# Denominators of latent attention from a column of ones in a third value product, rope tables in three transfers, a later load of x

## The chip, the cores and the metric

One Trainium2 chip, of which the kernel uses one core. The metric is the device time of one execution in microseconds, and a kernel is compared by its median over several executions.

## What is computed

The reference runs two transformer blocks over one sequence of 1024 tokens of width 1024, all in float32. The first mixes a pooling path and a sliding-window attention and adds the result to x; the second is a hybrid of latent attention (MLA, 8 heads, keys and queries of 96, values of 64) and three groups of dilated attention, with gates, an output product and a final norm. Cut to the part at issue:

```python
def mla_attention(c_q, c_kv, k_rope, positions, q_norm_g, kv_norm_g, w_uq, w_ukv):
    q = (rmsnorm_2(c_q, q_norm_g) @ w_uq).reshape(B, S, MLA_HEADS, MLA_QK_DIM)
    q = jnp.concatenate([q[..., :64], rope(q[..., 64:], positions)], axis=-1) * 96 ** -0.5
    kv = (rmsnorm_2(c_kv, kv_norm_g) @ w_ukv).reshape(B, S, MLA_HEADS, 64 + 64)
    k_nope, v = kv[..., :64], kv[..., 64:]
    k_pe = rope(k_rope[:, :, None, :], positions)          # shared by the heads
    s = jnp.einsum('bqhd,bkhd->bhqk', q, k)                # no mask
    return jnp.einsum('bhqk,bkhd->bqhd', jax.nn.softmax(s, axis=-1), v)

def first_block(x, ...):
    ...
    y = jnp.concatenate([pool_out, attn_out], axis=-1) @ w_out
    return x + rmsnorm(y, norm_post)

def rope(t, positions):      # cos and sin of position x frequency, 32 frequencies for 64, 16 for 32
    ...
```

## The kernel before

Every float32 product is made of three fast ones. A tensor is split into a high part, rounded to the matmul's type (an ACT copy), and a low part, the rest (a DVE subtraction, `sub_lo`, L119); then high x high, high x low and low x high are summed in one PSUM bank. Such a group of three is called a triple below (`mm3_lane`, lines L360 to L362). Projections go by tiles of 128 outputs by 512 tokens, 8 triples each.

The program has stages in this order: the first block (its output product with `y_lane`, which also loads x as `xt` and adds it, and which calls `rope_tables` at the second token tile); projections and dilated attention of the second block; the latent projections (`c_lane`: eight token tiles of c_q, c_kv and k_rope, then `ct_lane`, which transposes each normalized tile `cn` on PE); `uq_lane` and `ukv_lane`, which make queries, keys and values; the latent attention; the two output products into a merge, and the last product. The order on PE is written by a planner while the program is built: each lane is a generator that yields the events it needs, `Flow.run` always steps the lane of highest priority whose events are due by its own clock (0.23 us a product of 512 columns), and `Ring` objects stand for buffers. A lane can be put off with `at(us)` or with a later event; both put the numbers 20.0 and 2.5 into the latent projections. `stream_lane`, of the lowest priority, fills the rest with projections of the gates (`gate_item`, triples on `pp`); in the latent attention a meter, `pace`, lets through so many of its triples per key block. The order on ACT, DVE, POOL and SP comes from the scheduler of the tile framework, which also holds an instruction back until its buffer is free.

In the latent attention four lanes run over heads, halves of 512 queries and 8 blocks of 128 keys. `max_lane` multiplies keys and queries once to find each query's maximum, transposes it and sends it as `mt` by DMA into a row of the queries. `exp_lane` makes the scores in three products (L1646 to L1648) and, on ACT, the exponential (L1653) and its high part `E` (L1654); DVE makes the low part `pl` (L119). `hi_lane` multiplies `E` by the 128 columns of `vm` that hold the low and the high part of the values (L1683), and `lo_lane` multiplies `pl` by the high part and a column of ones beside it (L1696), into a second bank. So per key block there are two value products. The sum over keys of `E` and `pl` together is what divides the output. The share of `pl` is row 64 of `lo_lane`'s bank. The share of `E` is summed apart: POOL adds the eight `E` of a half head (L1664, L1666) into `acc`, and `key_sums` splits `acc` into a high and a low part `ehl` (ACT L1588, DVE L119), multiplies both with `ones` on PE (L1593, L1594, bank `psd`), copies the row (L1598) and stores it in `den_d`.

At the end of a half head the banks are copied and added: ACT copies `ot` (L1703), DVE adds (L1704), ACT copies `ou` (L1705), DVE adds again (L1706), and SP stores `ot` in `a_d` and ACT the row of `ou` in `den_d`. `ot`, `ou`, `den` and `mt` all come from one pool of two buffers:

```python
                nc.scalar.copy(t[0:64], o[64:128])
                nc.vector.tensor_tensor(out=t[0:64], in0=o[0:64], in1=t[0:64], op=ALU.add)
                nc.scalar.copy(u[0:65], o2[0:65])
                nc.vector.tensor_tensor(out=t[0:64], in0=t[0:64], in1=u[0:64], op=ALU.add)
```

`finish`, once per two heads, loads both rows of denominators, adds them, takes the reciprocal, spreads it by DMA, and multiplies the output on POOL. The merge then loads that as `raw`, splits it into `at`, and multiplies it by w_o (the first product on `at` ends the latent part).

`rope_tables` makes one cosine and two sine tables of 32 frequencies by 1024 positions, as tiles of 128 rows (4 quarters of the positions by 32 frequencies) by 256, and stores each to `cs_d` in four transfers (L579). `tables` reads 32-row slices for the dilated attention, and the lines behind L1368 16-row slices for the latent attention.

Of the kernel before, what the change touches and what calls it, by code (L numbers as in the profile page):

```python
# [14 lines left out]
S = 1024  # L15
# [52 lines left out]
def hybrid_kernel(  # L68
# [467 lines left out]
    cs_d = tc.dram_tile([3, 32, S], F32, name="cs_d")  # L536

    def rope_tables():
# [434 lines left out]
    def y_lane(t):  # L973
# [7 lines left out]
        xt = C("xt")  # L981
        nc.sync.dma_start(xt, x[128 * t:128 * t + 128, :])
# [32 lines left out]
    a_d = tc.dram_tile([512, S], F32, name="a_d")  # L1015
    ag_d = tc.dram_tile([512, S], F32, name="ag_d")
    den_d = tc.dram_tile([2, 8, S], F32, name="den_d")
# [43 lines left out]

    def z_item(o, dst, j, evs):
# [307 lines left out]
    for r in range(2):  # L1370
        nc.sync.dma_start(qtab[64 + 16 * r:80 + 16 * r], cs_d[0, 0:32:2])
        nc.sync.dma_start(qtab[96 + 16 * r:112 + 16 * r], cs_d[2 - r, 0:32:2])
        nc.sync.dma_start(ktab[16 * r:16 * r + 16], cs_d[0, 0:32:2])
        nc.sync.dma_start(ktab[32 + 16 * r:48 + 16 * r], cs_d[2 - r, 0:32:2])
# [26 lines left out]
    def c_lane():  # L1401
        yield (at(20.0),)
        for t in range(8):
# [17 lines left out]
            F.add(ct_lane(t, cn, Ev(slot.t + 2.5)), 4)  # L1421
# [104 lines left out]
    ones = cst.tile([128, 1], F32R, name="ones")  # L1526
    nc.vector.tensor_scalar(out=ones, in0=ident[:, 0:1], scalar1=0.0, scalar2=1.0, op0=ALU.mult, op1=ALU.add)
# [3 lines left out]
    den_ev = [[Ev(), Ev()] for _ in range(8)]  # L1531
# [51 lines left out]
    def key_sums(e, h, half, ready):  # L1583
        yield (ready, R.P)
        Pslot = R.P.take()
        ehl = P_p.tile([128, 2, 512], F32R, tag="P", name="ehl")
        eh, el = ehl[:, 0], ehl[:, 1]
        nc.scalar.copy(eh, e)  # L1588
        sub_lo(nc.vector, el, e, eh)
        yield (R.S, Ev(F.chain(("a", 0.6), ("v", 1.3)) + 3.0))  # L1590
        slot = R.S.take()
# [296 lines left out]
```

## Time and profile before

| | us |
|---|---|
| runs | 1740.76, 1731.06, 1731.16 |
| median | 1731.16 |
| the profiled execution | 1742.75 |
| its span, first to last instruction | 1740.7 |
| its mean granted clock of TensorE | 0.977 of full speed |

A row of groups names the line, the engine, the operation, what it writes and reads, the shapes and the count; then busy time, the mean duration, and the idle time of the engine just before with what ended it. In a timeline row the first number is the start, the second the duration, and what stands in brackets is how long the engine was idle before it and what released it. Line numbers are those of the kernel before.

### The profile page before, as it was taken

The numbers are of one execution on the slowest core, as the hardware profiler recorded it, in microseconds if no ns is written. First come the engines' busy times: TensorE is split into PE (matmuls) and PEld (weight loads), VectorE is DVE, ScalarE is ACT, GpSimd is POOL, SyncE is SP. The second block draws the span as 40 slices with busy tenths as digits, with TensorE's granted clock in tenths as the row PEclk, the third lists the DMA queues.
The fourth block names the chain that finished last, engine by engine and source line by source line (L and its number), as shares of the span: only waits on it lengthen the run. The fifth ranks groups of instructions, "written<-read, shape, count | busy, mean of one in ns | idle before, by whom it ended". The sixth has DMA issues, their size and how long they took to land.

```text
span 1740.7 us, 22397 instructions
## 1 busy us (share of the span) xinstructions
PE 1647.7 (95%) x7892; PEld 1355.4 (78%) x7892; DVE 1016.3 (58%) x1912; ACT 798.0 (46%) x1659; POOL 394.2 (23%) x336
## 2 busy tenths in 40 slices
PE   6999997999999999999999988899998989999998
PEld 6888876788788788888888777887766767777786
DVE  6587693453566646665555663365676767545432
ACT  5465533332455545655444442315665656742121
POOL 2000020000000000000000444452566566622200
PEclk9999998999999999999999999999999999999999
DMA  6111224534443443334345668354223231378542
GB/s 193 49 49 39 69 91 141 157 116 121 98 96 80 100 118 87 80 88 116 94 101 115 156 168 215 89 173 150 57 76 103 58 104 48 103 243 289 160 139 80
DMA packets 214092, 200.59 MB, mean 115 GB/s; under 512 B 50451, under 2 KB 177299, under 8 KB 212444
## 3 DMA queue, kind: packets, MB, share of 16 engines
q1 hardware_dynamic: 210780, 188.55, 39.4%
q10 hardware_dynamic: 3200, 10.62, 1.7%
q8 instruction: 62, 1.02, 0.2%
q14 instruction: 50, 0.41, 0.1%
HBM read 124.73 MB, written 48.11 MB: 99 GB/s over the span
## 4 chain that ended last, share of the span: by engine, by line
PE 46%; DMA 8%; DVE 7%; ACT 5%; SPq 4%; issue 3%; POOL 2%; DVEq 0%; POOLq 0%; ACTq 0%
PE pp L360 8%; PE pp L362 8%; PE pp L361 8%; DMA rsw<-rt 3%; SPq L1185 2%; PE pso L493 2%; PE y L361 2%; PE y L362 2%; PE y L360 2%; PE pss L1646 1%; PE pso L1696 1%; PE pst L463 1%; PE pss L1648 1%; PE pss L1647 1%; PE pso L1683 1%
## 5 line engine op out<-in xcount | busy, mean ns | idle before, releaser
L360 PE MATMUL pp<-Hh,whi 128*128 128x512 f32 x1248 | 504.7, 404 | 11.8 <-DVE pg L588 5.9
L362 PE MATMUL pp<-Hh,wlo 128*128 128x512 f32 x1248 | 492.8, 395 | 0.0
L361 PE MATMUL pp<-Hl,whi 128*128 128x512 f32 x1248 | 492.0, 394 | 0.0
L360 PEld LDWEIGHTS pp<-Hh,whi 128*128 128x128 f32 x1248 | 238.6, 191 | 57.7 <-DVE pg L588 6.8
L362 PEld LDWEIGHTS pp<-Hh,wlo 128*128 128x128 f32 x1248 | 237.0, 190 | 52.5
L361 PEld LDWEIGHTS pp<-Hl,whi 128*128 128x128 f32 x1248 | 238.2, 191 | 42.4
L127 ACT CAST whi<-wraw 128x1024 fp32r<-128x1024 f32 (+1 forms) x108 | 109.2, 1011 | 198.7 <-PE pp L361 95.6
L119 DVE TENSOR_TENSOR wlo<-wraw,whi 128x1024 fp32r<-128x1024 f32 (+1 forms) x108 | 135.2, 1252 | 100.4 <-ACT whi L127 91.0
L1666 POOL TENSOR_TENSOR acc<-acc,E 128x512 f32<-128x512 f32 x96 | 132.0, 1375 | 84.3 <-ACT E L1654 81.5
L443 ACT ACTIVATE P<-P,nm 128x256 f32<-128x256 f32 (+2 forms) x256 | 118.8, 468 | 59.4 <-DVE nm L438 59.2
L119 DVE TENSOR_TENSOR pl<-pss,E 128x512 fp32r<-128x512 f32 x128 | 86.9, 686 | 67.4 <-ACT E L1654 66.4
L1653 ACT ACTIVATE pss<-pss 128x512 f32<-128x512 f32 x128 | 74.9, 588 | 70.7 <-PE pss L1648 62.3
L1567 DVE TENSOR_REDUCE mx<-pst 128x1 f32<-128x512 f32 x128 | 83.6, 682 | 19.1 <-PE pst L1565 18.6
L119 DVE TENSOR_TENSOR pl<-pst,ph 128x512 fp32r<-128x512 f32 (+2 forms) x120 | 75.3, 639 | 32.0 <-ACT ph L469 31.4
L432 DVE CUSTOM_DVE_ANT_0 P<-pss,cc 128x256 f32<-128x256 f32 (+2 forms) x192 | 62.9, 369 | 45.8 <-PE pss L1145 45.7
L167 POOL TENSOR_TENSOR rs<-ms,mhalf 128x1 f32<-128x1 f32 (+1 forms) x40 | 25.0, 626 | 273.0 <-DVE ms L165 272.9
L469 ACT CAST ph<-pst 128x512 fp32r<-128x512 f32 (+2 forms) x120 | 63.9, 551 | 33.2 <-PE pst L463 32.1
L1654 ACT CAST E<-pss 128x512 fp32r<-128x512 f32 x128 | 74.2, 588 | 2.8
L493 PE MATMUL pso<-pl,v 128*128 128x256 f32 (+1 forms) x280 | 71.7, 286 | 1.6 <-DVE pl L119 1.6
L493 PE MATMUL pso<-ph,v 128*128 128x256 f32 (+1 forms) x280 | 72.0, 286 | 0.1
L1186 DVE TENSOR_TENSOR rsw<-rsw,tab 128x1024 f32<-128x1024 f32 x24 | 29.4, 1224 | 72.8 <-DMA rsw<-rt 72.8
L502 ACT COPY ot<-pso 64x512 f32<-64x512 f32 x64 | 37.4, 584 | 72.3 <-PE pso L493 71.7
(273 smaller groups left out, 3163.6 us busy)
## 6 DMA issues: line engine op xcount, KB each, us to landing
wraw<-in_w_in_dram SPq DMA_DIRECT2D x78, 512.0 KB
rsw<-rt SPq DMA_DIRECT2D x96, 128.0 KB
ksd<-ksd SPq DMA_DIRECT2D x24, 512.0 KB
wraw<-in_w_out_dram SPq DMA_DIRECT2D x16, 512.0 KB
g_d<-g ACTq DMA_DIRECT2D x16, 512.0 KB
og_d<-ot SPq DMA_DIRECT2D x48, 128.0 KB
ol<-og_d SPq DMA_DIRECT2D x24, 256.0 KB
ol<-b_d SPq DMA_DIRECT2D x48, 128.0 KB
```

Of the source, the lines that this page charges most:

```text
L119: eng.tensor_tensor(out=lo, in0=src, in1=hi.bitcast(F32), op=ALU.subtract)
L127: nc.scalar.copy(wh, raw)
L360: nc.tensor.matmul(ps, lh, rh, start=(i == 0), stop=False)
L361: nc.tensor.matmul(ps, lh, rl, start=False, stop=False)
L362: nc.tensor.matmul(ps, ll, rh, start=False, stop=(i == n - 1))
L443: nc.scalar.activation(out=a, in_=a, func=AF.Exp, bias=nm[:, i:i + 1], scale=hd.scale, accum_out=hd.den[:, i:i + 1])
L469: nc.scalar.copy(ph[:, :w], ps[:, :w])
L493: nc.tensor.matmul(o[b][:, q0:q0 + 128 * w], hd.v(c), part[:, cols + 128 * x:cols + 128 * (x + w)], start=b not in opened, stop=(part is p ...
L1567: nc.vector.tensor_reduce(out=mx[:, n, i:i + 1], in_=ps, axis=mybir.AxisListType.X, op=ALU.max)
L1653: nc.scalar.activation(out=ps, in_=ps, func=AF.Exp, scale=MSC)
L1654: nc.scalar.copy(ph, ps)
L1666: nc.gpsimd.tensor_tensor(out=acc, in0=acc, in1=ph.bitcast(F32), op=ALU.add)
```

## The change

The value products become three. `hi_lane` multiplies `E` by the 65 columns of high values and ones, into the first bank, and by the 64 columns of low values, into the second. `lo_lane` multiplies `pl` by the same 65 columns, into the first bank too. Row 64 of the first bank is then the whole denominator. POOL's sums, `key_sums`, `den_d` and the second output copy and sum go; `a_d` gets 65 rows per head, and `finish` loads output and denominators from it, in two transfers each. The ring of `pl` buffers has 6 places instead of 4.

Apart from that: the tables of rope are stored in one transfer each, in another layout, and read in pieces of 1 KB; `y_lane` asks for x before the second half of its product instead of before the first; the latent projections begin 4 us later by the planner's clock and their transposes 2.5 us later. Two functions are added that nothing calls (`spare_gate`, `filler_lane`).

```diff
-    cs_d = tc.dram_tile([3, 32, S], F32, name="cs_d")
+    cs_d = tc.dram_tile([3, 4, 32, 256], F32, name="cs_d")
...
-            for c in range(4):
-                nc.sync.dma_start(cs_d[n][:, 256 * c:256 * c + 256], t[32 * c:32 * c + 32])
+            nc.sync.dma_start(cs_d[n].rearrange("c f t -> (c f) t"), t)
...
-        xt = C("xt")
-        nc.sync.dma_start(xt, x[128 * t:128 * t + 128, :])
...
         for n in range(2):
             c = tokens(n)
+            if n:
+                xt = C("xt")
+                nc.sync.dma_start(xt, x[128 * t:128 * t + 128, :])
...
-    a_d = tc.dram_tile([512, S], F32, name="a_d")
+    a_d = tc.dram_tile([8, 65, S], F32, name="a_d")
...
-                nc.sync.dma_start(u[32 * r:32 * r + 32], cs_d[n * (2 - r % 2)])
+                nc.sync.dma_start(quarters(u[32 * r:32 * r + 32]), table(n * (2 - r % 2)))
...
     def c_lane():
-        yield (at(20.0),)
+        yield (at(24.0),)
...
-            F.add(ct_lane(t, cn, Ev(slot.t + 2.5)), 4)
+            F.add(ct_lane(t, cn, Ev(slot.t + 5.0)), 4)
...
-    def key_sums(e, h, half, ready):
...
     def finish(j):
...
-        nc.sync.dma_start(a, a_d[row])
-        rd2 = sm.tile([128, 2, 16], F32, tag="rd2", name="rd2", bufs=2)
+        rd = sm.tile([128, 16], F32, tag="rd2", name="rd2", bufs=2)
         for i in range(2):
-            nc.sync.dma_start(rd2[:, i], den_d[i, 2 * j:2 * j + 2].rearrange("h s -> (h s)").rearrange("(p n) -> p n", n=16))
-        rd = rd2[:, 0]
-        nc.vector.tensor_tensor(out=rd, in0=rd, in1=rd2[:, 1], op=ALU.add)
+            nc.sync.dma_start(a[64 * i:64 * i + 64], a_d[2 * j + i, 0:64])
+            nc.sync.dma_start(rd[64 * i:64 * i + 64], a_d[2 * j + i, 64].rearrange("(p n) -> p n", n=16))
...
-    R.pl, R.mx = Ring(4), Ring(3)
+    R.pl, R.mx = Ring(6), Ring(3)
...
-                    pl = pt_p.tile([128, 512], F32R, tag="ph" if kb % 4 == 3 else "pl", name="pl")
+                    pl = pt_p.tile([128, 512], F32R, tag="ph" if kb % 2 else "pl", name="pl")
...
-                    if kb == 1:
-                        acc = pt_p.tile([128, 512], F32, tag="ph", name="acc")
-                        nc.gpsimd.tensor_tensor(out=acc, in0=E[:, 0].bitcast(F32), in1=E[:, 1].bitcast(F32), op=ALU.add)
-                    elif kb > 1:
-                        nc.gpsimd.tensor_tensor(out=acc, in0=acc, in1=ph.bitcast(F32), op=ALU.add)
...
-                    nc.tensor.matmul(o, vm[:, kb, h, 0:128], parts[h, half, kb][0], start=(kb == 0), stop=(kb == 7))
-                    F.mm(1)
+                    ph = parts[h, half, kb][0]
+                    nc.tensor.matmul(o[0:65], vm[:, kb, h, 64:129], ph, start=(kb == 0), stop=False)
+                    nc.tensor.matmul(o2[0:64], vm[:, kb, h, 0:64], ph, start=(kb == 0), stop=(kb == 7))
+                    F.mm(2)
...
-                    nc.tensor.matmul(o2[0:65], vm[:, kb, h, 64:129], pl, start=(kb == 0), stop=(kb == 7))
+                    nc.tensor.matmul(o[0:65], vm[:, kb, h, 64:129], pl, start=False, stop=(kb == 7))
...
-                u = ot_p.tile([128, 512], F32, tag="ot", name="ou")
-                nc.scalar.copy(t[0:64], o[64:128])
-                nc.vector.tensor_tensor(out=t[0:64], in0=o[0:64], in1=t[0:64], op=ALU.add)
-                nc.scalar.copy(u[0:65], o2[0:65])
-                nc.vector.tensor_tensor(out=t[0:64], in0=t[0:64], in1=u[0:64], op=ALU.add)
-                nc.sync.dma_start(a_d[64 * h:64 * h + 64, c], t[0:64])
-                nc.scalar.dma_start(den_d[1, h:h + 1, c], u[64:65])
+                nc.scalar.copy(t[0:65], o[0:65])
+                nc.vector.tensor_tensor(out=t[0:64], in0=o2[0:64], in1=t[0:64], op=ALU.add)
+                nc.sync.dma_start(a_d[h, :, c], t[0:65])
```

Counted over the whole order, PE has 7964 products instead of 7868. Up to the latent projections nothing on it changes. There, 33 stream triples stand ahead of the first product of `c_lane` that stood behind 27; the third pair of transposes stands behind 40 triples of `c_lane` instead of 36. Between the last value product and the first product on `at` stand 172 products instead of 201.

On PE, in the latent attention, the rows before (L1683 is the high value product, L1696 the low one, L360 to L362 a gate's triple, L1646 the scores of the next key block):

```order
L1696 MATMUL pso_10889<-pl,vm 65x512
L1683 MATMUL pso<-E,vm 128x512
L360 MATMUL pp<-Hh,whi 128x512
L361 MATMUL pp<-Hl,whi 128x512
L362 MATMUL pp<-Hh,wlo 128x512
L1683 MATMUL pso<-E,vm 128x512
L1696 MATMUL pso_10889<-pl,vm 65x512
L1646 MATMUL pss<-qh,kh 128x512
```

and of the changed kernel at the same place (L1684 and L1685 are the two high products, L1698 the low one, L1655 to L1657 the scores):

```order
L1684 MATMUL pso<-E,vm 65x512
L1685 MATMUL pso_10911<-E,vm 64x512
L1698 MATMUL pso<-pl,vm 65x512
L1655 MATMUL pss<-qh,kh 128x512
L1656 MATMUL pss<-ql,kh 128x512
L1657 MATMUL pss<-qh,kl 128x512
L1698 MATMUL pso<-pl,vm 65x512
L1684 MATMUL pso<-E,vm 65x512
L1685 MATMUL pso_10911<-E,vm 64x512
```

The low product has moved into the bank of the first high product, and each high product is followed by a second one.

On ACT, at the change from one head to the next, the rows before (L1653 is an exponential, L1654 the cast of its high part, L1576 makes `mt`, L1580 sends it, L1703 and L1705 are the output copies, L1050 a gate's tanh):

```order
L1653 ACTIVATE pss<-pss 128x512
L1576 ACTIVATE mt<-pst 8x128
L1654 CAST E<-pss 128x512
L1580 DMA qh<-mt 1x8x128
L1580 DMA ql<-mt 1x8x128
L1653 ACTIVATE pss<-pss 128x512
L1703 COPY ot<-pso 64x512
L1654 CAST E<-pss 128x512
L1653 ACTIVATE pss<-pss 128x512
L1705 COPY ou<-pso_12131 65x512
L1050 ACTIVATE g<-pp,bgate 128x512
L1654 CAST E<-pss 128x512
```

and of the changed kernel (L1662, L1663, L1608, L1612, L1704 and L1056 in the same parts; L127 is the cast of a weight tile):

```order
L1662 ACTIVATE pss<-pss 128x512
L1704 COPY ot<-pso 65x512
L1662 ACTIVATE pss<-pss 128x512
L1608 ACTIVATE mt<-pst 8x128
L1663 CAST E<-pss 128x512
L127 CAST whi<-wraw 128x1024
L1056 ACTIVATE g<-pp,bgate 128x512
L1663 CAST E<-pss 128x512
L1612 DMA qh<-mt 1x8x128
L1612 DMA ql<-mt 1x8x128
```

The copy `ou` behind the transfer of `mt` is gone; a weight cast and a tanh now stand together between two casts of `E`.

On POOL, in the latent projections around the copies for the third token tile, the rows before (acc and ol are the merge of the dilated groups, rs the norm's factor, cn the two copies that the transposes wait for):

```order
L1343 TENSOR_TENSOR acc<-acc,ol 128x512
L1342 TENSOR_TENSOR ol<-ol 128x512
L167 TENSOR_TENSOR rs<-ms,mhalf 128x2
L1340 TENSOR_TENSOR acc<-ol 128x512
L1343 TENSOR_TENSOR acc<-acc,ol 128x512
L1342 TENSOR_TENSOR ol<-ol 128x512
L1418 COPY cn<-cn 128x16
L1419 COPY cn<-cn 128x16
```

and of the changed kernel (its lines are 35 higher):

```order
L1453 COPY cn<-cn 128x16
L1454 COPY cn<-cn 128x16
L1375 TENSOR_TENSOR acc<-ol 128x512
L1378 TENSOR_TENSOR acc<-acc,ol 128x512
L167 TENSOR_TENSOR rs<-ms,mhalf 128x2
L1377 TENSOR_TENSOR ol<-ol 128x512 x2
L1453 COPY cn<-cn 128x16
L1454 COPY cn<-cn 128x16
```

The factor rs has moved behind the two acc rows, and there are two ol rows ahead of the third tile's copies instead of one.

## Rows read from the trace of the kernel before

**Rows 1.** The page, engine totals: busy us (share of the span) x instructions.
```profile
PE 1647.7 (95%) x7892; PEld 1355.4 (78%) x7892; DVE 1016.3 (58%) x1912; ACT 798.0 (46%) x1659; POOL 394.2 (23%) x336
```

**Rows 2.** Windows: start:end us, PE, PEld, DVE, ACT, POOL busy, PEclk, DMA share, GB/s.
```profile
1075.00:1123.00 48.00, 41.80 (x221) 40.02 (x221) 16.15 (x38) 12.76 (x51) 19.93 (x32) 0.93 0.49 122
1222.00:1530.00 308.00, 289.60 (x1187) 214.73 (x1186) 204.49 (x311) 199.42 (x355) 194.64 (x128) 0.97 0.28 79
```

**Rows 3.** Windows of 20 us in the latent attention.
```profile
1260.00:1280.00 20.00, 18.45 (x78) 13.29 (x77) 17.90 (x30) 11.64 (x22) 12.86 (x9) 1.00 0.40 100
1320.00:1340.00 20.00, 16.76 (x60) 12.24 (x59) 7.71 (x11) 12.49 (x23) 14.91 (x10) 0.83 0.19 51
1340.00:1360.00 20.00, 17.87 (x68) 12.73 (x68) 17.80 (x26) 9.45 (x17) 10.13 (x8) 0.91 0.39 99
```

**Rows 4.** Waits of PE, 1222 to 1530: us in total, times, longest us.
```profile
PE pso L1696 <- DVE pl L119: 10.8, 7, 2.4
PE pso L1683 <- ACT E L1654: 6.9, 6, 3.2
```

**Rows 5.** Timeline of PE in the latent attention.
```profile
1227.09 0.40 PE L1696 MATMUL pso<-pl,vm 128*65 128x512 f32 x1
...
1230.60 0.40 PE L1565 MATMUL pst<-kh,qh 96*128 96x512 f32 x1
...
1267.05 0.45 PE L1696 MATMUL pso<-pl,vm 128*65 128x512 f32 x1 [1.41 <-DVE pl L119]
...
1348.09 0.45 PE L1696 MATMUL pso<-pl,vm 128*65 128x512 f32 x1 [1.87 <-DVE pl L119]
```

**Rows 6.** Timeline of ACT at a change of heads.
```profile
1323.97 0.58 ACT L1705 COPY ou<-pso 65x512 f32<-65x512 f32 x1 [3.69 <-DMA ql<-mt]
```

**Rows 7.** Timeline of DVE ahead of the wait at 1265.6.
```profile
1261.90 0.96 DVE L1706 TENSOR_TENSOR ot<-ot,ou 64x512 f32<-64x512 f32 x1
...
1265.12 0.68 DVE L119 TENSOR_TENSOR ehl<-acc,ehl 128x512 fp32r<-128x512 f32 x1
```

**Rows 8.** Groups by line and shape, whole span, and for ACT 1222 to 1530.
```profile
L1666 POOL TENSOR_TENSOR acc<-acc,E 128x512 f32<-128x512 f32 x96 | 132.0, 1375 | 84.3 <-ACT E L1654 81.5
L1706 DVE TENSOR_TENSOR ot<-ot,ou 64x512 f32<-64x512 f32 x16 | 18.0, 1123 | 8.4 <-ACT ou L1705 8.3
L1050 ACT ACTIVATE g<-pp,bgate 128x512 f32<-128x512 f32 x17 | 11.7, 688 | 1.4 <-PE pp L362 1.4
L127 ACT CAST whi<-wraw 128x1024 fp32r<-128x1024 f32 x8 | 8.4, 1050 | 2.4 <-PE pp L361 2.4
```

**Rows 9.** Timelines of PE and POOL in the latent projections.
```profile
1099.19 0.52 PE L1429 MATMUL pst<-idt,cn 128*128 128x128 f32 x3 [1.72 <-DVE cn L1415]
1103.72 0.42 PE L1430 MATMUL pst<-idt,cn 128*64 128x128 f32 x1 [4.01 <-POOL cn L1419]
...
1101.88 1.51 POOL L1342 TENSOR_TENSOR ol<-ol 128x512 f32<-128x512 f32 x1
1103.34 0.20 POOL L1418 COPY cn<-cn 128x16 f32<-128x16 f32 x1
```

**Rows 10.** Timelines of PE and SP at the end of the first block's inner stage.
```profile
279.23 0.80 PE L360 MATMUL pp<-Hh,whi 128*128 128x512 f32 x1 [5.88 <-DVE pg L588]
...
262.45 5.81 SPq L579 DMA_DIRECT2D cs_d<-rp  x6
```

**Rows 11.** Timelines of PE, DVE and SP at the end of the latent attention.
```profile
1527.93 0.39 PE L1696 MATMUL pso<-pl,vm 128*65 128x512 f32 x1
...
1575.38 0.39 PE L360 MATMUL pp<-at,whi 128*128 128x512 f32 x1
...
1567.38 1.22 DVE L119 TENSOR_TENSOR at<-raw,at 128x1024 fp32r<-128x1024 f32 x1
...
1535.81 0.50 SPq L1607 DMA_DIRECT2D a<-a_d  x1
1540.29 0.32 SPq L1610 DMA_DIRECT2D rd<-den_d  x1
```

More of the change, by code (lines that the diff above doesn't have):

```diff
@@ L533, in grouped, with table, quarters @@
         return ap if g == 0 else ap.rearrange("p (r l) -> p r l", r=RES[g])
-    cs_d = tc.dram_tile([3, 32, S], F32, name="cs_d")
+    cs_d = tc.dram_tile([3, 4, 32, 256], F32, name="cs_d")
+    def table(n, rows=slice(0, 32)):
+        return cs_d[n].rearrange("c f t -> f c t")[rows]
+    def quarters(ap):
+        return ap.rearrange("f (c t) -> f c t", c=4)
     def rope_tables():
@@ L1060, in gate_item, with spare_gate, evac, f @@
         return pair_item(w2(O_GM, j), f, H2, H2h)
+    def spare_gate(j):
+        def evac(half):
+            def f(ps):
+                t = ot_p.tile([128, 512], F32, tag="ot", name="gt")
+                nc.scalar.activation(out=t, in_=ps, func=AF.Tanh, scale=0.5, bias=bgate[:, j:j + 1])
+                nc.scalar.dma_start(g_d[128 * j:128 * j + 128, tokens(half)], t)
+                return F.chain(("a", 0.7))
+            return f
+        return pair_item(w2(O_GM, j), evac, H2, H2h)
+    spare_on = [True]
+    def filler_lane(items):
+        while items and spare_on[0]:
+            yield (R.W,)
+            if not spare_on[0]:
+                return
+            it = items.pop()
+            slot, w, ready = R.W.take(), it.loads[0](), F.load()
+            for (_, rhs, evac, need) in it.parts:
+                yield (R.pp, ready) + tuple(need)
+                bank = R.pp.take()
+                ps = pp.tile([128, 512], F32, tag="pp", name="pp")
+                yield from paced(ps, [((w[0][:, k], w[1][:, k]), r) for k, r in enumerate(rhs)])
+                bank.t = evac(ps)
+            slot.t = F.now
     def z_item(o, dst, j, evs):
@@ L1370, in hybrid_kernel @@
     for r in range(2):
[L1371 to L1374, printed above, removed]
+        nc.sync.dma_start(quarters(qtab[64 + 16 * r:80 + 16 * r]), table(0, slice(0, 32, 2)))
+        nc.sync.dma_start(quarters(qtab[96 + 16 * r:112 + 16 * r]), table(2 - r, slice(0, 32, 2)))
+        nc.sync.dma_start(quarters(ktab[16 * r:16 * r + 16]), table(0, slice(0, 32, 2)))
+        nc.sync.dma_start(quarters(ktab[32 + 16 * r:48 + 16 * r]), table(2 - r, slice(0, 32, 2)))
     def ps_s():
@@ L1581, in max_lane @@
             qk_ev[h].t = slot.t + 2.2
-    def key_sums(e, h, half, ready):
[L1584 to L1591, printed above, removed]
-        ps = psS.tile([128, 512], F32, tag="s", name="psd")[0:1]
-        nc.tensor.matmul(ps, ones, eh, start=True, stop=False)
-        nc.tensor.matmul(ps, ones, el, start=False, stop=True)
-        F.mm(2)
-        Pslot.t = F.now
-        d = ot_p.tile([128, 512], F32, tag="ot", name="den")[0:1]
-        nc.scalar.copy(d, ps)
-        slot.t = F.chain(("a", 0.6))
-        nc.scalar.dma_start(den_d[0, h:h + 1, tokens(half)], d)
-        den_ev[h][half].t = slot.t + 2.2
     def finish(j):
@@ L1636, in exp_lane @@
                 c = tokens(half)
-                acc = None
                 for kb in range(8):
@@ L1660, in exp_lane @@
                     parts[h, half, kb] = (ph, pl, pslot, Eslot)
-                    if kb == 1:
-                        acc = pt_p.tile([128, 512], F32, tag="ph", name="acc")
-                        nc.gpsimd.tensor_tensor(out=acc, in0=E[:, 0].bitcast(F32), in1=E[:, 1].bitcast(F32), op=ALU.add)
-                    elif kb > 1:
-                        nc.gpsimd.tensor_tensor(out=acc, in0=acc, in1=ph.bitcast(F32), op=ALU.add)
-                    if kb:
-                        e1 = F.chain(("g", 1.3), at=e1)
-                F.add(key_sums(acc, h, half, Ev(e1)), 7)
     outs = {}
```

8 lines of the change are left out of this document (2 added, 6 removed).

## Prediction

> **What bounds the kernel now.** I read the page's engine totals first, then windows by stage, then the waits of PE in the two stages that the change touches, then timelines around the longest of them. PE is busy 1647.7 of 1740.7 us [rows 1], so 93.0 us are idle in the whole span, and a gain can only come from there or from stretches at half clock. The stage of the latent attention, 1222 to 1530, has 308.00 - 289.60 = 18.4 us of idle, and a granted clock of 0.97; the stage of the latent projections, 1075 to 1123, has 48.00 - 41.80 = 6.2 us and 0.93 [rows 2]. Everywhere else a product added is simply time added.
>
> In the attention stage the waits have two names [rows 4]: 10.8 us on `pl`, the low half of the exponentials that DVE makes, in 7 waits, and 6.9 us on `E`, ACT's high half, in 6. What each looks like is in two timelines. At 1265.6 PE waits 1.41 us [rows 5] while DVE does a last sum of the output, L1706, in 0.96 us and the low half of the key sums in 0.68 before the `pl` that PE wants [rows 7]. At 1323.97 ACT's copy `ou` has waited 3.69 us for the transfer of `mt`, since `mt` and `ou` share the two `ot` buffers [rows 6]; the E cast queued behind that copy is late, and PE's 3.2 us are the longest of the E waits [rows 4]. So both waits are made by work that the sums of the denominators bring: POOL's 96 running sums, DVE's ehl and L1706, ACT's ou.
>
> The clock: after the 1.41 us wait it stays at 1.00, that is 2.4 GHz, in 1260 to 1280; after the longer ones it falls to 1.2 GHz for some us, 0.83 in 1320 to 1340 and 0.91 in three more windows, of which one stands there [rows 3]. Half clock costs (0.17 + 3 x 0.09) x 20 = 8.8 us of full speed.
>
> **What the change costs and gives.** *Products.* 128 high products become 256, 32 key sum products go: +96. Fifteen starts from 1227.09 to 1230.60 lie 0.234 us apart [rows 5]; that the new ones have 65 and 64 columns changes nothing, since the low product with 65 has the pitch of those with 128. +96 x 0.234 = **+22.5 us**, all on PE's path. The Trainium skill ("TensorE: Matmul & The Clock Gate", Back-to-back issue gap) gives a sustained 131 ns for a product of 512 columns, and by it the estimate would be 12.6 us and the sum 10 lower; the trace does not agree, it has 0.234 in an unbroken run, and I go by that.
>
> *Waits of the attention stage.* Removed from DVE: 16 subtractions for ehl and, of the two sums per half head, one, the L1706 at 1.123; from POOL, 96 sums at 1.375 [rows 8] and 16 first ones; from ACT, the ou copies and the ehl casts. The `ot` pool then has three users per head instead of seven, so a copy no longer takes the buffer that `mt` still holds. What stands next in the queue: at each head's boundary the order of ACT now has a weight cast (1.050 us) and a gate's tanh (0.688) between E casts [rows 8]. That makes an E late by up to 1.74, and a PE that has other products to do meets perhaps a third of it: 0.6 us in 8 heads, about 5. Bounds: nothing left (0), and as now (18.4), or above that if the low products, which now end the same bank as the high ones, wait longer. I take 5, nearer the low end because the queue work removed is what ended both kinds of waits: 18.4 - 5 = **-13.4 us**. With no wait as long as 1.87 the clock has no cause to fall: **-8.8 us**, between 0 and 8.8.
>
> *Latent projections.* The third pair of transposes waits 1.72 us for DVE's `cn`, then 4.01 for POOL's copies, which start at 1103.34 [rows 9] behind the dilated merge's acc and ol. Six stream triples more ahead of the first c product, and four more c triples ahead of the third transposes, are 18 x 0.234 + 12 x 0.19 = 6.5 us (0.19 is 0.234 x 416/512, the columns of a c product) by which PE arrives later, with work that has to be done anyhow. POOL's order however now has the rs and a second ol, 1.51 us, between the sums and that copy: at the durations of before it starts some 2.3 us later, near 1105.7, and PE, which began to wait at 1099.19 - 1.72 = 1097.5, would begin at 1104.0. With the 0.4 us from copy to product, 2.2 us are left of 5.7: -3.5. The clock's 0.07 x 48 = 3.4 us of loss [rows 2] I halve: -1.7. Together **-5.2 us**; bounds 0 and -9.1.
>
> *Rope tables.* Twelve writes of cs_d become three; in the first block's last stage six of them sit on SP for 5.81 us ahead of a weight load for the output projection, and PE then waits 5.88 us [rows 10]; the releaser named there is another engine's row, so that the load is behind it is my reading. Most of the 5.81 can only be SP waiting for the tables, since an issue takes 0.3 to 0.45 [rows 11]. Four or so issues go from ahead of that load, 1.8 us, and I take a third of it as met by PE: **-0.6 us**, between -3 (half of the wait) and +1 (the three writes are larger). The reads in 1 KB pieces fill tables that POOL copies or DVE reads much later, and x, asked for before the second half of a token tile, has that half's 24 products, 5.6 us, to arrive while PE goes on with the next tile; I put both at nothing, and a late x at 1 us per tile of DVE's time, which no product waits for before the last tile.
>
> *End.* From the last value product, 1527.93, to the first product on `at`, 1575.38, PE works through 201 matmuls; now 172. The filling shrinks to 172 x 0.234 = 40.2 us. The chain beside it: the last `at` is split by 1567.38 + 1.22 = 1568.6, 40.7 us after the value product; the step of it that changes is the second load of the denominators, issued at 1540.29, where the load of `a` went at 1535.81 [rows 11]; the denominators now lie in a_d, so they can go with it, 4.5 us earlier. 40.7 - 4.5 = 36.2: the cover holds by 4 us. Were the chain as long as now, PE would wait 0.5. The load of `a` is now two transfers to two halves of the partitions; the Trainium skill ("DMA: Bandwidth & Descriptors", Rules for kernel authors) says that such a pair runs one after the other and should be one transfer. No run here shows it. By it the load would come later by one issue, within the cover.
>
> Sum: 22.5 - 13.4 - 8.8 - 5.2 - 0.6 = **-5.5 us** against the profiled execution's 1742.75, that is 1737.2. The median of the runs, 1731.16, lies 11.6 below the profiled execution; so some of the idle seen here is absent in a usual run. The idle credited, 13.4 + 3.5 + 0.6 = 17.5, is 19% of the 93.0; I take the same share of 11.6, 2.2 us, as gone already. That leaves -3.3: **1728 us**. If all 11.6 were of what is credited, it would be 1731.16 - 5.5 + 11.6 = 1737.
>
> **Rivals.** *Waits come back at head boundaries* (the slower side). Place: ACT's queue at the head change, the weight cast and tanh between E casts. If they make PE idle for 1.87 us or more, as before the product at 1348.09, where the clock then fell [rows 3, 5], each of 7 boundaries costs 1.9 us of idle and 1.7 of half clock: 25 instead of 5, so 1728 + 20 = 1748. It decides from a wait between 1.41, which left the clock alone, and 1.87. For it: before, the same tanh and cast sit near the same waits. Against: PE has gate triples and score products in between, and the ou copy, which held ACT longest, is gone.
>
> *The latent projections gain nothing*, because the copies on POOL stay behind transfers for the merge: +5.2, 1733. For it: the two ol rows ahead of the copy, and waits for b_d that don't depend on PE.
>
> *All of it pays*: no wait in the attention stage (-5) and the full 9.1 (-3.9): 1719. For it: 7 of 13 waits end on DVE, which loses 18.0 us of L1706 [rows 8] and 16 subtractions of 0.68 or more [rows 7], while POOL loses 132.0 [rows 8]. Against: a wait of ACT's queue is left at each boundary.
>
> **How the numbers follow.** My case has a chance of 0.60 and holds 1716 to 1742; the waits at the head boundaries 0.17 at 1748, spread 1738 to 1760; no gain in the projections 0.08; all of it pays 0.15, spread 1708 to 1722. About what a measurement can tell from no change is 1%: faster is below 1713.8, slower above 1748.5. Below 1713.8 lie a quarter of the best case and a twentieth of mine: 0.04 + 0.03, 0.08 with rounding up. Above 1748.5 lie half of the first rival and a twentieth of mine: 0.085 + 0.03, 0.12. The rest is 0.80. The range from 1713 to 1750 leaves out about 0.08 on the low side and 0.10 on the high side.
>
> **What would show it.** PE has 96 more products in the attention stage; its idle falls from 18.4 to near 5, and no 20 us window there has a clock under 0.95. `pl` as a releaser of PE drops below 3 us. The E waits, if any, come behind a weight cast or a tanh. In the latent projections POOL's copies still end one wait, of some 2 us. The first `at` product does not wait. The prediction is wrong if the attention stage grows by more than the added products less 15 us, or if a new name ends PE's waits, such as the a_d store, or the `pso` bank at a head's change.

## The result, and the profile after

The changed kernel takes 1716.21 us (median of 4 runs, 1715.64 to 1721.41); the kernel before, in runs of the same chip, 1735.96 (4 runs, 1731.06 to 1742.57). The ratio is 0.990, with a 95% interval of 0.9869 to 0.993: some 17 us faster. A second series gave 0.9915 (0.9894 to 0.9935), some 15 us. The direction and the range of the prediction hold, the size doesn't: it had 1728, and 3 us of gain. Three executions in the series below took far longer than the rest (1834.76, 1841.69 and 3226.08 us); the ratios leave them out, the medians don't.

The engine totals, to set beside [rows 1]:

```profile
PE 1643.7 (96%) x7988; PEld 1354.5 (79%) x7988; DVE 980.1 (57%) x1875; ACT 769.3 (45%) x1611; POOL 235.9 (14%) x224
```

PE has its 96 products more, and the span is 1713.8 us. The windows, with the columns of [rows 2]: the latent projections, the latent attention, and 20 us within it as in [rows 3].

```profile
1065.00:1120.00 55.00, 50.99 (x265) 47.61 (x264) 17.21 (x36) 17.15 (x61) 22.88 (x35) 0.97 0.55 128
...
1209.00:1506.00 297.00, 296.98 (x1281) 218.77 (x1280) 177.64 (x280) 173.77 (x312) 44.31 (x19) 1.00 0.30 87
...
1300.00:1320.00 20.00, 20.00 (x88) 14.89 (x87) 13.97 (x23) 12.68 (x23) 4.77 (x2) 1.00 0.64 179
```

The attention stage has no idle left (297.00 - 296.98) and no half clock; the view of PE's waits is empty there, where [rows 4] had 17.7 us. This is so although ACT's queue at a head's change reads as the order said: a weight cast and a tanh between two casts of E.

```profile
1273.27 0.56 ACT L1663 CAST E<-pss 128x512 fp32r<-128x512 f32 x1
...
1273.73 1.04 ACT L127 CAST whi<-wraw 128x1024 fp32r<-128x1024 f32 x1
...
1274.68 0.68 ACT L1056 ACTIVATE g<-pp,bgate 128x512 f32<-128x512 f32 x1
...
1276.25 1.04 ACT L1663 CAST E<-pss 128x512 fp32r<-128x512 f32 x2
```

The next E comes 2.4 us later, and no product waits for it.

To find the stages I cut both traces at the same products: the first and last of each kind that the order names. Between the cuts stand the time, and what of it is idle by the profile or lost to half clock (half the time at 1.2 GHz). The idle time ahead of PE's first product and behind its last one is left out.

| up to | before: us | idle, clock | after: us | idle, clock | products more |
|---|---|---|---|---|---|
| last product of the first block's output | 399.39 | 23.8, 10.2 | 392.80 | 21.4, 10.2 | 0 |
| last score product of the dilated attention | 626.68 | 22.0, 12.0 | 620.95 | 21.1, 8.5 | 0 |
| first product of the latent projections | 49.20 | 6.6, 5.1 | 51.18 | 5.6, 3.4 | 18 |
| last transpose of the latent projections | 54.84 | 6.2, 3.4 | 54.90 | 4.0, 1.7 | 9 |
| first value product | 93.03 | 0.9, 0 | 89.63 | 0.1, 0 | -9 |
| last value product | 304.80 | 18.4, 8.5 | 296.88 | 0.0, 0 | 107 |
| first product on `at` | 47.45 | 0.8, 0 | 43.60 | 3.7, 0 | -29 |
| end | 165.27 | 2.2, 1.2 | 163.84 | 2.8, 2.5 | 0 |

The sum is -26.9 us, more than the medians say. The 5.7 us in the dilated attention are no more than this part differs by between executions of kernels that are alike there, and the profile of before was taken in one of its longer executions (experiment 1).

### The profile page after: what moved, and what is told of

It is laid out like the page before. It is cut to its first block, busy times and chain, and to the rows that moved or that the text cites. A ratio compares the mean times of both kernels' runs of the same rounds, so it can differ in the third digit from the quotient of the medians.

```text
span 1713.8 us, 22215 instructions
## 1 busy us (share of the span) xinstructions
PE 1643.7 (96%) x7988; PEld 1354.5 (79%) x7988; DVE 980.1 (57%) x1875; ACT 769.3 (45%) x1611; POOL 235.9 (14%) x224
## 4 chain that ended last, share of the span: by engine, by line
PE 70%; DMA 10%; DVE 6%; SPq 4%; ACT 4%; issue 3%; POOL 2%; DVEq 0%; POOLq 0%; ACTq 0%
PE pp L360 12%; PE pp L361 12%; PE pp L362 12%; PE y L361 3%; PE y L362 3%; PE y L360 3%; PE pso L493 3%; DMA rsw<-rt 3%; PE pst L463 2%; SPq L1220 2%; PE pso L1698 2%; PE pss L1655 2%; PE pso L1684 2%; PE pss L1657 2%; PE pss L1656 2%
## 5 line engine op out<-in xcount | busy, mean ns | idle before, releaser
L360 PE MATMUL pp<-Hh,whi 128*128 128x512 f32 x1248 | 503.7, 404 | 10.2 <-DVE pg L594 4.5
L362 PE MATMUL pp<-Hh,wlo 128*128 128x512 f32 x1248 | 490.7, 393 | 0.0
L360 PEld LDWEIGHTS pp<-Hh,whi 128*128 128x128 f32 x1248 | 237.6, 190 | 56.7 <-DVE pg L594 5.5
L362 PEld LDWEIGHTS pp<-Hh,wlo 128*128 128x128 f32 x1248 | 236.5, 190 | 52.1
L119 DVE TENSOR_TENSOR wlo<-wraw,whi 128x1024 fp32r<-128x1024 f32 (+1 forms) x108 | 131.3, 1215 | 100.6 <-ACT whi L127 95.4
L127 ACT CAST whi<-wraw 128x1024 fp32r<-128x1024 f32 (+1 forms) x108 | 109.1, 1010 | 174.4 <-PE pp L361 77.3
L1662 ACT ACTIVATE pss<-pss 128x512 f32<-128x512 f32 x128 | 74.1, 582 | 111.4 <-PE pss L1657 102.2
L469 ACT CAST ph<-pst 128x512 fp32r<-128x512 f32 (+2 forms) x120 | 63.8, 550 | 32.9 <-PE pst L463 31.9
L1663 ACT CAST E<-pss 128x512 fp32r<-128x512 f32 x128 | 72.8, 586 | 1.9
L463 PE MATMUL pst<-idt,P 128*128 128x128 f32 x440 | 67.4, 274 | 2.6 <-ACT P L443 2.3
L502 ACT COPY ot<-pso 64x512 f32<-64x512 f32 x64 | 37.4, 584 | 70.2 <-PE pso L493 69.5
L1179 PE MATMUL pss<-ksd,qs 128*128 128x256 f32 (+2 forms) x192 | 50.0, 287 | 15.2 <-DVE qs L119 15.2
```

The costliest lines, as they stand in the source:

```text
L119: eng.tensor_tensor(out=lo, in0=src, in1=hi.bitcast(F32), op=ALU.subtract)
L127: nc.scalar.copy(wh, raw)
L360: nc.tensor.matmul(ps, lh, rh, start=(i == 0), stop=False)
L362: nc.tensor.matmul(ps, ll, rh, start=False, stop=(i == n - 1))
L463: nc.tensor.transpose(ps[:, w:w + 128], hd.P[i // 4][:, i % 4, p0:p0 + 128], ident)
L469: nc.scalar.copy(ph[:, :w], ps[:, :w])
```

## The experiments

Ratios are to the kernel before in the same series. "The stage" is the time from the first to the last value product.

**1. The kernel before, a second profile.** No edit.

> The kernel before once more, for a second profile. The profiles of before and after differ by 26.9 us of span, of which 6.6 lie ahead of the end of the first block's output product, 5.9 in the dilated attention, whose instructions the change hardly touches, and 16.5 behind the first product of the latent projections. Theory A: the first two are made by the change, so this profile repeats that of before: first block's output product ends near 399.4 us, dilated stage 562 us, span near 1740. Theory B: some of it is variation between executions of one kernel (its runs lie near 1731 and near 1741): then this profile may have a span near 1730, with the dilated stage near 556 or the output product ending near 393.

One execution, 1738.27 us. Its span is 1736.2, with the first block's output product ending at 398.4, dilated attention 559.9 from its first score product (562.2 in the first profile). Over all profiles of this study that part takes 555.6 to 566.0, with 6.8 to 16.5 us lost to half clock, in kernels with the change as in those without. So executions differ there, and one profile each is no measure of it. The attention stage repeats: idle 18.9, stage 302.98, with 5.1 us lost to half clock instead of 8.5.

**2, 3. Rope tables alone; the later load of x alone.** The hunks of the diff on `cs_d`, or the one on `xt`, put into before.

> Before, with the rope tables alone in three transfers and read in 1 KB pieces. Theory A: the nine writes that go from SP's queue bring the weight loads of the output product forward, the waits of 5.88 and 3.27 us before it shrink to about 4.5 and 1.8, and the end of that product comes 4 to 7 us earlier: ratio 0.996 to 0.998. Rival: the later load of x does that, and this kernel is equal to before within 1 us in that stage. The dilated stage stays within 2 us of before if the 1 KB reads don't matter, and is 6 us shorter if they do.

> Before, with the load of x in the output stage of the first block moved behind the first half of each product, and nothing else. Theory A (rope writes make the gain there): within 1 us of before in that stage, ratio 0.999 to 1.001. Rival (x loads stood ahead of weight loads on SP): the end of the output product comes 2 to 6 us earlier, ratio 0.997 to 0.999.

Rope tables: 1734.86, 0.9993 (0.9971 to 1.0015), and the output product ends at 400.0: nothing. The dilated attention of this execution takes 555.6, the 6 us less that I had tied to the reads of 1 KB; but the kernel of experiment 6, without them, has 556.2, and kernels with them have up to 566.0, so it isn't shown to be theirs. The load of x: 1730.11, 0.9977 (0.9953 to 1.0001), output product ending at 397.7. PE's two waits ahead of that product, in the kernel with the rope tables, with the later x, and in the changed kernel:

```profile
279.40 0.79 PE L360 MATMUL pp<-Hh,whi 128*128 128x512 f32 x1 [5.87 <-DVE pg L594]
...
298.05 0.68 PE L360 MATMUL y<-wo,whi 128*128 128x512 f32 x1 [3.35 <-issue]
```

```profile
279.80 0.80 PE L360 MATMUL pp<-Hh,whi 128*128 128x512 f32 x1 [5.74 <-DVE pg L588]
...
297.53 0.47 PE L360 MATMUL y<-wo,whi 128*128 128x512 f32 x1 [1.98 <-issue]
```

```profile
278.29 0.51 PE L360 MATMUL pp<-Hh,whi 128*128 128x512 f32 x1 [4.54 <-DVE pg L594]
...
294.55 0.47 PE L360 MATMUL y<-wo,whi 128*128 128x512 f32 x1 [1.75 <-issue]
```

The later x shortens the second wait: it is 1.7 to 2.1 us in the nine profiles of this study with the later x and 2.7 to 3.4 in the five without. Its load no longer stands on SP ahead of the mix and weight loads; that this is the reason is my reading. The first wait is less clear: 4.2 to 5.8 us in the seven kernels with both edits and the stores on SP, 5.1 to 6.2 in the four with neither.

**4. Denominators alone.** All hunks on `a_d`, `den_d`, `key_sums`, `finish`, `hi_lane`, `lo_lane` and the ring.

> Before, with the denominators from the third value product alone (pl ring of 6 with it); rope tables, x and the start of the latent projections as before. Theory A: the latent attention has 107 more products than before between its first and last value product and yet no idle and no half clock (before 18.4 us and 8.5 us), so the gain behind the latent projections, 14 to 16 us, is all here: ratio 0.990 to 0.993. Rival: that stage's waits went because the latent projections were put off, then here waits of 5 us or more are left and the ratio is 0.995 or more.

1726.82, 0.9955 (0.9939 to 0.9971). The stage takes 296.5 us with 0.6 idle and no half clock, so its waits go by this part alone. The gain behind the last transpose of the projections is 7.3 us and not the 14 to 16 that I had written; the changed kernel has 16.6 there. It has 27 products fewer behind that transpose, 6.3 us: they stand ahead of it.

**5. The changed kernel with the latent projections begun as before.**

```diff
-        yield (at(24.0),)
+        yield (at(20.0),)
...
-            F.add(ct_lane(t, cn, Ev(slot.t + 5.0)), 4)
+            F.add(ct_lane(t, cn, Ev(slot.t + 2.5)), 4)
```

> The changed kernel with the latent projections begun as before: 20.0 and 2.5 in place of 24.0 and 5.0. Theory A: the later start lets work that must be done anyway fill the wait for POOL's copies, and it keeps gate triples out of the attention's end; the profile of before shows 5.7 us of waits at the third transposes, 1.4 us of waits fewer and half the clock loss in the changed one, so this kernel is 3 to 6 us slower than the changed one (ratio to before 0.992 to 0.994). Rival: the start only moves triples from one stage to another, and the ratio stays at 0.990 within 0.001.

1720.94, 0.9922 (0.9902 to 0.9941). Its projections take 54.89 us for 9 products fewer, idle 5.9 and 3.4 of half clock, as before; the delay gives back 3.6 us of these. In the ratios it is 4 us against the first series of the changed kernel and 1 against the second (0.9915), with intervals that overlap: a gain of the whole kernel from the delay is not shown. From experiment 4 to this one, which adds rope tables and x together and has the same order on PE, it is 0.9955 to 0.9922, 5.7 us.

**6. mt in a place of its own, in before.**

```diff
-            t = ot_p.tile([128, 2, 256], F32R, tag="ot", name="mt")[0:8, :, 0:128]
+            t = cc[0:8, 0:256].bitcast(F32R).rearrange("p (n q) -> p n q", n=2)
```

> Before, with the negated maxima mt in a place of their own (rows of a constant tile that nothing reads any more) in place of one of the two ot buffers. Theory A: the waits of PE on ACT's E (6.9 us in 6 waits before) are made by the ou copy that waits for mt's transfer; they fall below 3 us, the wait of ou on DMA ql<-mt (6.0 us) is gone, and the stage has one or two stretches of half clock fewer: 5 to 9 us less, ratio 0.995 to 0.997. The waits on DVE's pl (10.8 us) stay above 7 us. Rival: E is late for ACT's own queue, and both waits stay as they are, ratio 1.000.

1734.19, 0.9987 (0.996 to 1.0015): not faster. ACT's copy `ou` no longer waits for the transfer of `mt`, where it waited 6.0 us in all in before, 5.8 and 6.8 in experiments 1 and 2, and 3.4 in 3. But PE's waits in the attention stage stay:

```profile
PE pso L1696 <- DVE pl L119: 8.4, 7, 1.6
PE pso L1683 <- ACT E L1654: 5.9, 6, 1.9
```

The order on PE is that of before, so the waits can be compared product by product. The two that came behind `ou` are gone (3.24 and 1.82 us in before, 1.0 to 3.2 in experiments 1 to 3). In their stead two of 1.91 and 1.88 us stand 66 products later, where before has 0.17 and none. There the cast of E stands on ACT behind the cast of the key sums, and that waits for POOL's last sum; the first of the two:

```profile
1338.15 0.62 ACT L1588 CAST ehl<-acc 128x512 fp32r<-128x512 f32 x1 [2.50 <-POOL acc L1666]
...
1338.68 0.58 ACT L1654 CAST E<-pss 128x512 fp32r<-128x512 f32 x1
...
1339.31 0.51 PE L1683 MATMUL pso<-E,vm 128*128 128x512 f32 x1 [1.91 <-ACT E L1654]
```

So the shared buffer did make the wait on which I had read the mechanism, and one more; without it the next step of the denominators in ACT's queue makes one of nearly that length.

**7, 8. The changed kernel with POOL's sums put back, and with four places for pl.** In both `Ring(6)` is `Ring(4)`, with the tags of before; in the first also the removed lines on `acc`, whose result nothing reads.

> The changed kernel with POOL's running sums of E put back as before, read by nothing, and with them the four pl places of before. Only POOL's work and its reads of E come back; DVE's and ACT's extra steps stay away. Theory A (DVE's and ACT's own queues made the waits): the latent attention keeps under 3 us of idle, within 2 us of the kernel with four places and no sums. Rival (POOL's sums slow DVE down, or hold E): DVE's low halves and copies take longer, their means rise by a tenth or more, and 5 to 12 us of waits on pl come back.

> The changed kernel with four places for pl, as before, in place of six. Theory A: the places don't matter, the waits of before came from queues; ratio 0.989 to 0.991, under 2 us of idle in the latent attention. Rival: the two added places are what lets the score products run ahead, and with four 4 to 10 us of waits on pl come back (0.993 to 0.996).

With POOL's sums: 1719.99, 0.9918 (0.9894 to 0.9943), stage 298.9, idle 0.9. With four places alone: 1726.99, 0.994 (0.9897 to 0.9983), stage 300.5, idle 2.0, none of it on `pl`. With four places the planner writes another order on PE, the same in both. So POOL's 147 us (190 busy in the stage against 43) cost nothing in this kernel, and the places with their order at most 3.6 us of the stage. DVE's groups in the stage, with POOL's sums and then in the changed kernel:

```profile
L119 DVE TENSOR_TENSOR pl<-pss,E 128x512 fp32r<-128x512 f32 x128 | 87.2, 688 | 99.0 <-ACT E L1663 95.5 <-PE pss L1656 3.2
...
L119 DVE TENSOR_TENSOR wlo<-wraw,whi 128x1024 fp32r<-128x1024 f32 x8 | 12.5, 1563 | 2.6 <-ACT whi L127 1.8 <-PE pss L1657 0.8
```

```profile
L119 DVE TENSOR_TENSOR pl<-pss,E 128x512 fp32r<-128x512 f32 x127 | 85.6, 687 | 83.5 <-ACT E L1663 83.0
...
L119 DVE TENSOR_TENSOR wlo<-wraw,whi 128x1024 fp32r<-128x1024 f32 x8 | 9.8, 1226 | 1.3 <-ACT whi L127 1.3
```

**9. POOL's sums and their split on ACT and DVE.** To experiment 7 comes, per half head, the cast and the subtraction of `key_sums` in a place of E's ring, without its products.

> The kernel with POOL's sums put back, and with it the split of those sums into a high and a low half on ACT and DVE in a place of E's ring, as before; no products of them, and nothing reads them. Theory A (the ACT and DVE steps of the key sums, one of each per half head, and the place they take from E made the waits): 5 us of idle or more come back in the latent attention, with waits on pl or E of 1 us and more. Rival (the waits came from the two further output steps, the copy ou and the sum L1706 of before, which stay away here): idle stays under 2 us, the stage within 2 us of that with POOL's sums alone.

1730.76, 0.9969 (0.9953 to 0.9986). The stage, and the waits of PE from 1525 to 1580:

```profile
1208.00:1509.00 301.00, 297.99 (x1274) 217.57 (x1273) 187.57 (x294) 180.42 (x324) 192.15 (x130) 1.00 0.28 82
```

```profile
PE pp L360 <- DVE gd L1765: 6.4, 1, 6.4
PE pp L360 <- DVE gm L1765: 2.9, 1, 2.9
```

Neither theory: 3.0 us idle, the stage 302.5, and 9.3 us of waits for gd and gm, DVE's gating steps, at the merge in place of 4.9 in the changed kernel. At the merge `gd` stands on DVE behind the split of the last `at`, which comes 36.9 us after the last value product and not 31.6:

```profile
1546.81 1.23 DVE L119 TENSOR_TENSOR at<-raw,at 128x1024 fp32r<-128x1024 f32 x1 [8.78 <-ACT at L1746]
1547.96 0.68 DVE L1765 SCALAR_TENSOR_TENSOR gd<-gd,pp 128x512 f32<-128x512 f32 x1
```

Against experiment 7 (0.9918) the whole kernel is some 9 us slower, with intervals that don't meet: 3.6 us in the stage and 6.6 from the last value product to the first on `at`. So the split, with the order that the planner gives it, costs half of the change's gain; the stage's waits of before it brings back only in small part.

**10, 11. The changed kernel again; and with two edits more.**

```diff
-            nc.sync.dma_start(cs_d[n].rearrange("c f t -> (c f) t"), t)
+            nc.scalar.dma_start(cs_d[n].rearrange("c f t -> (c f) t"), t)
...
-            nc.gpsimd.tensor_copy(out=kk[:, 1, 0], in_=kk[:, 0, 1])
-            nc.gpsimd.tensor_copy(out=kk[:, 1, 1], in_=kk[:, 0, 0])
+            nc.vector.tensor_copy(out=kk[:, 1, 0], in_=kk[:, 0, 1])
+            nc.vector.tensor_copy(out=kk[:, 1, 1], in_=kk[:, 0, 0])
```

> The changed kernel once more, to be set beside the next one on the same chip: 1714 to 1722 us, ratio to before 0.989 to 0.992, no idle over 1 us and no half clock in the latent attention, and the first block's output product ending within 2 us of 392.8.

> The changed kernel with the three writes of the rope tables issued by ACT, which makes the tables, in place of SP, and with the two small cn copies of the latent projections on DVE in place of POOL. Theory A: SP's weight loads of the output product stood 5 us behind the third table; they go at once, the wait before the output product falls from 4.5 us to under 1.5, the wait for POOL's copies (1.3 us) goes, and with a stretch or two of half clock that is 4 to 8 us less than the changed kernel: ratio to before 0.985 to 0.988. Rival: the loads come earlier, but the next weight tile or the table load of ACT is then what PE waits for, and it stays within 2 us of the changed kernel.

1721.20, 0.9915 (0.9894 to 0.9935), and 1719.02, 0.9905 (0.9882 to 0.9929). In the second the output product ends at 390.5 instead of 394.0, and the projections take 51.0 instead of 55.4, without half clock:

```profile
276.26 0.50 PE L360 MATMUL pp<-Hh,whi 128*128 128x512 f32 x1 [3.92 <-DVE pg L594]
...
292.61 0.47 PE L360 MATMUL y<-wo,whi 128*128 128x512 f32 x1 [1.75 <-issue]
```

```profile
1073.00:1123.00 50.00, 48.19 (x258) 45.37 (x257) 19.66 (x52) 16.31 (x60) 20.16 (x19) 1.00 0.51 124
```

That is 8 us in these two stages against this execution of the changed kernel, and 4 against the shortest of either stage in the other kernels with both edits; the dilated attention of the same execution is 4.7 longer, and the medians differ by 2.2 with intervals that overlap. Whether it beats the changed kernel is not shown. The first wait fell to 3.9 only, from 4.2 to 5.8 in the kernels with the stores on SP, so most of it is something else than the third table's write.

**12. The changed kernel without the third product.** Left out is E times the low half of the values, so the output is not the right one:

```diff
-                    nc.tensor.matmul(o2[0:64], vm[:, kb, h, 0:64], ph, start=(kb == 0), stop=(kb == 7))
-                    F.mm(2)
+                    F.mm(1)
...
-                nc.vector.tensor_tensor(out=t[0:64], in0=o2[0:64], in1=t[0:64], op=ALU.add)
+                nc.vector.tensor_tensor(out=t[0:64], in0=o[0:64], in1=t[0:64], op=ALU.add)
```

> The changed kernel without the product of E with the low half of the values (128 of them; the output lacks that half, and the last sum adds the first bank to its own copy). From the first to the last value product stand 1151 products instead of 1279. Theory A (the waits of before ended because queue work of ACT, DVE and POOL went): no idle comes back, the stage is 128 x 0.233 = 29.8 us shorter than the changed kernel's 296.9, near 267, ratio to before 0.972 to 0.976. Rival (the third product itself is what fills the waits, as PE has more of its own to do while ACT and DVE make E and pl): with it gone 10 us of idle or more come back, with some half clock, the stage is 275 us or longer and the ratio 0.978 or more; then the third product costs far less than its 0.233 each.

1706.12, 0.9832 (0.9802 to 0.9863). The stage takes 277.5 us:

```profile
1221.00:1497.00 276.00, 273.84 (x1146) 198.48 (x1145) 174.43 (x279) 170.45 (x309) 42.91 (x18) 1.00 0.33 93
```

The rival's stage and ratio came, not its idle column or its half clock. 128 products fewer save 296.9 - 277.5 = 19.4 us, 0.152 each and not 0.233. Some 10 us come back as short waits: counted from the starts of the products, as in the next section, 10.9 us instead of 1.6, of which the profile calls 2.2 idle. The clock stays full.

## Why the prediction was right in its direction, and wrong in its size

That the time lies in the range is luck in part. The prediction counted from a median of 1731.16; the ratio of 0.990 on that is 1713.8, at the very edge of the range from 1713, and it is before's median of 1735.96 in the comparison that leaves the result at 1716. By the experiments the gain of 15 to 17 us is 8 us for the denominators (4), 6 for rope tables and x together (4 to 5) and 1 to 4 for the delay, not shown by itself (5).

**The waits of the attention stage were mis-sized**: "I take 5, nearer the low end", and 18.4 as what there was. Left were 0.0; and the 18.4 were too few. A product's row lasts 0.40 us while products start 0.234 apart [rows 5], so of each wait 0.16 us lie under the row of the product before it, and a wait shorter than that is not idle at all. Taken from the starts of the products (outside half clock, what each interval has above 0.2335): in before, about 23 intervals of 0.40 or more hold 22.1 us of waiting and 39 between 0.245 and 0.40 another 3.0; after, 1 and 22 hold 1.6. So 25.1 us were to be had, not 18.4, and with half clock 7.8 more by the same count. Over five profiles with the products of this stage as they were (the first, 1, 2, 3, and 6 with `mt` apart) it takes 296.7 to 309.3, on the mean 302.6; with the change, three times (the first, 10 and 11), 296.9. With 107 products more, 25.0 us, the waits and the clock gave 30.7 on the mean (24.7 to 37.4 by the single profiles), where I had credited 22.2. That is the larger part of the error. Experiment 4 agrees within its interval: its stage has 95 products more and takes 296.5, which makes 302.6 + 22.2 - 296.5 = 28.3, and 22.4 - 28.3 = -5.9 us for its 96 products in all; measured are -7.8 (-10.6 to -5.0).

**The products** cost what they were to cost: 296.88 us for 1279 products is 0.232 each. But not all of it is added time: without the third product some 10 of its 30 us would be waits (12).

**The clock**: right. No wait in the stage, no fall. The bounds of 1.41 and 1.87 us did not hold in other executions: the clock stayed at full speed after waits of 2.10 (1) and 1.87 (3), and fell after one of 1.61 (6).

**The mechanism**: the rows bear it out more widely than I had read it, but how much each step is worth stays open. In before all ten waits over 0.5 us have a removed step close ahead of what ends them, in the same engine's queue: six of the seven on `pl` the low half of the key sums on DVE, with no idle time from there to `pl`; the seventh the second output sum; two on E the copy `ou` that waits for `mt`; the third the cast of the key sums, which waits 0.98 for POOL. The seventh on `pl`:

```profile
1421.24 2.87 DVE L1706 TENSOR_TENSOR ot<-ot,ou 64x512 f32<-64x512 f32 x1
1424.04 0.67 DVE L119 TENSOR_TENSOR pl<-pss,E 128x512 fp32r<-128x512 f32 x1
...
1424.77 0.45 PE L1696 MATMUL pso<-pl,vm 128*65 128x512 f32 x1 [0.91 <-DVE pl L119]
```

That sum takes 2.87 us where it can take 0.68. Both output sums of before, with the shortest, median and longest in ns:

```profile
L1704 DVE TENSOR_TENSOR ot<-pso,ot x16: 675/683/683, 1243.5 to 1528.8; 64x512 f32<-64x512 f32 x16
L1706 DVE TENSOR_TENSOR ot<-ot,ou x16: 683/958/2874, 1245.6 to 1529.5; 64x512 f32<-64x512 f32 x16
```

The five L1706 that meet less than 0.2 us of POOL's work take 0.68, the eleven others 0.81 to 2.87. So POOL's sums did lengthen a step ahead of `pl`. Experiment 7 could not show it, since that step is gone there: it shows only that the sums by themselves cost nothing in the changed kernel. In the same way 8 and 9 were put under a third product that covers waits, and say what a step costs there: the places a few us of the stage (8, where the ratio's interval holds the changed kernel's), the split 3.6 of the stage and 9 of the whole (9). The filling by the third product is worth some 10 us (12). Without it 10.9 us of waits are left of 32.9 in before (25.1 and 7.8), so the larger part went with the removed steps, the two places and the order that came with them. The second output copy and sum, and the products and copies of the key sums, were not put back alone, and no removed step was put back without the third product, so how that part divides is open.

**Rope tables and x**: the tables' -0.6 is within what was measured (nothing). My "nothing" for x was wrong for its wait (2, 3). That the two edits need each other is not shown: alone they give 1.2 and 4.0 us by the ratios, each within its interval of nothing, and together 5.7 from experiment 4 to 5. The output product ends at 392.1 to 395.1 in the seven profiles with both and the stores on SP, at 400.0 and 397.7 with one, and at 396.0 to 401.2 in the four with neither. What sets the first wait is not settled.

**Latent projections**: -5.2 foreseen; idle and clock fell by 2.2 + 1.7 = 3.9 in the one profile of each. The third transposes do still wait for POOL behind two ol rows, and a wait at the second ones came new:

```profile
1087.21 0.57 PE L1464 MATMUL pst<-idt,cn 128*128 128x128 f32 x3 [1.75 <-ACT krT L1469]
...
1095.07 0.30 PE L1465 MATMUL pst<-idt,cn 128*64 128x128 f32 x1 [1.33 <-POOL cn L1454]
```

```profile
1090.67 1.56 POOL L1377 TENSOR_TENSOR ol<-ol 128x512 f32<-128x512 f32 x1
1093.23 1.51 POOL L1377 TENSOR_TENSOR ol<-ol 128x512 f32<-128x512 f32 x1 [1.00 <-DMA ol<-b_d]
1094.68 0.20 POOL L1453 COPY cn<-cn 128x16 f32<-128x16 f32 x1
```

**The end**: the cover held, with more to spare than foreseen. As in [rows 11]:

```profile
1506.35 0.39 PE L1698 MATMUL pso<-pl,vm 128*65 128x512 f32 x1
...
1549.96 0.39 PE L360 MATMUL pp<-at,whi 128*128 128x512 f32 x1
...
1510.88 0.59 SPq L1622 DMA_DIRECT2D rd<-a_d  x1
...
1537.94 1.23 DVE L119 TENSOR_TENSOR at<-raw,at 128x1024 fp32r<-128x1024 f32 x1 [4.19 <-ACT at L1727]
```

The second load of the denominators goes 4.5 us after the last value product (12.4 before), and `at` is ready 32.8 after it, not 36.2; PE needs it at 43.6. What I had not foreseen are 4.9 us of waits for gd and gm, DVE's gating steps, of which 2.9, for gd, lie within the filling; before has 0.3 there.

**The scale**: that 19% of the credited idle is absent from a median run was drawn from three runs with a median of 1731.16. The later series of before have medians of 1733.8 to 1736.6, so the three shown lay low, and the correction of 2.2 us was drawn from too few runs.

**The rivals**: waits at head boundaries did not come, though the order is as foreseen. "All of it pays", 1719, was the nearest, and I had given it 0.15.

## What to carry to other kernels

Before crediting a wait, take it from the starts of the products and not from the idle column: where rows overlap, each wait is longer by the overlap, and the short ones don't show. Work added to the bound engine is cheaper than its duration where that engine waits on a chain beside it, and where several steps stand in the queues that it waits for, taking away the one behind the longest wait may only let the next one through (6). Put each removed step back alone before giving it the credit, and without the cover that came with the change: under that cover a step shows what it costs there, not what it cost before. Where one stage varies by 10 us between executions, compare stages over several profiles, cut at the same products.

## What was not expected

In 7 POOL's sums lengthen DVE's subtraction on a weight tile, whose operands are all in SBUF, from 1.226 to 1.563 us on the mean (1.225 with the four places alone), but not each time: in 9, beside the same sums, five of eight stay at 1.23. The subtraction that reads scores from PSUM stays at 0.688 against 0.687, as the output sum L1704 of before, which reads PSUM too, stays at 0.68 beside them. And a stage at 94% busy had more to give than its idle column said: with 107 products more the stage takes 5.7 us less on the mean.
